# A hybrid two-layer encoder on one core: planner priorities, the place of a neighbourhood unit, key lows in zero-padded tiles, and like matmuls together

## The chip, the cores and the metric

The kernel runs on one core of one Trainium2 chip. The time is that of one execution on the device, in microseconds (us), and smaller is better. One run of the kernel is profiled: each instruction of each engine with its start and its duration. TensorE is called PE in the profile (its weight loads PEld), VectorE DVE, ScalarE ACT, GpSimd POOL, and SyncE, which only issues DMAs here, SP.

## What is computed

512 tokens of width 1024 go through two layers. In each layer the normed input `h` is multiplied by one wide matrix, and its parts go three ways: neighbourhood attention (16 heads on a grid of 8 x 64 tokens), dilated attention (24 heads in three groups with dilations 1, 4 and 16, mixed by their log-sums) and a bidirectional state-space model (24 heads, chunks of 128 tokens). The three results are projected, gated and merged, and a gated embedding is added. All inputs are float32.

```python
for i in range(DEPTH):
    h = rms_norm(x, norm_w[i])
    (qa, ka, va, ga, qb, kb, vb, gb, xbc, z, dt_raw, ua, ub, uc) = [
        h @ w for w in jnp.split(w_in[i], split_idx, axis=1)]
    ya = neighbourhood_attention(split_heads(qa, NA_HEADS), split_heads(ka, NA_HEADS),
                                 split_heads(va, NA_HEADS), na_rpb[i]).reshape(b, s, NA_WIDTH)
    ya = (ya * jax.nn.silu(ga)) @ w_oa[i]
    ...
    yb = dilated_mixture(qbh, kbh, split_heads(vb, DIL_HEADS)).reshape(b, s, DIL_OUT_WIDTH)
    yb = (yb * jax.nn.silu(gb)) @ w_ob[i]
    yc = mamba2_bidirectional(xbc, z, dt_raw, conv_w[i], conv_b[i], a_log[i], dt_bias[i],
                              d_skip[i], ssm_norm_w[i]) @ w_oc[i]
    merged = jax.nn.sigmoid(ua) * ya + jax.nn.sigmoid(ub) * yb + jax.nn.sigmoid(uc) * yc
    x = x + merged @ w_out[i]
    gate = jax.nn.sigmoid(rms_norm(x, ple_norm_w[i]) @ w_ple_gate[i])
    x = x + (p[i] @ w_ple[i]) * gate
return rms_norm(x, final_norm_w)
```

## The kernel before

**Two steps.** The kernel is first recorded and then ordered. `Emit` calls engine methods in program order; each call becomes a `Node` with a number `i`, its engine, its tiles and its predecessors (`Recorder.add`, L222). `Recorder.schedule` (L267) then plays the program through with a table of costs (`cost`, L151) and gives each engine a fixed order of its own; `emit` writes the instructions in that order. On the chip every engine works through its order strictly from front to back and waits at whatever isn't ready. All instructions are written from one place, so nearly all rows of the profile carry L261, and the names of the tiles tell them apart.

**How the planner chooses** (L309 to L340). Each time an engine is free in its play, it takes from the ready nodes the one with the lowest number, if that lies within 2500 places of the first node not yet placed (`WINDOW`) and if `fits` (L392) finds room in the pools for the tiles that it is the first to use. The pools: up to 55 tiles of 2 KB per partition with the tag `t` (`NT`, L432), three each of `raw`, `whi` and `wlo`, and in PSUM three `pj`, two `sc`, two `tr` and one `av` (L440).

**Matmuls in three terms.** Weights come as float32 blocks of 128 x 1024 on SP's queue (`fetch`, L444). `block` (L450) splits each into a high part `whi` (ACT copies with rounding) and a low part `wlo` (DVE subtracts); activations are split likewise (`hh` and `hl`, `yh` and `yl`). A product is then three matmuls, high by high, low by high and high by low (`mm3`, L460). A projection (`proj`, L469) is a block, 24 matmuls of 512 columns into one `pj` tile, and its reader on ACT or DVE.

**The stages of a layer** stand in `ORDER` (L1248), one word for each: `N0` to `N3` are neighbourhood units of four heads (`na_unit`, L1074), `S0` to `S3` state-space groups (`ssm_group`, L760), `O0` and `O1` the halves of the output product of the state-space path (`out_c`, L848), `G` its gates, `D0` and `D1` halves of the dilated attention (`dil_half`, L887), `A` and `B` the merges, and `L` the stores that were put off (`stores`, L1243). Before them stand the norm and the rows of dt (`dt_rows`, L656), behind them `tail` (L1181).

**Scores.** `stack` (L1109) builds for a pair of heads two query tiles `qs` (64 rows of high part, 64 of low part for each head), two key tiles `ks` (the high part twice), and one tile `kl` that holds the low parts of the keys, head 0 in rows 0 to 63 and head 1 in rows 64 to 127. `scores` (L969) makes for two heads and two blocks one matmul over all 128 rows of `qs` and `ks`, and then one over the 64 rows that a head owns in `kl`. The softmax follows on DVE and ACT, four transposes on PE (`turn`, L983) and the product with the values into `av`, whose matmuls write 64 rows of PSUM for each head.

**A state-space pair** (`ssm_pair`, L776) is long on DVE: four convolution steps `cv`, the products `cx`, `z` and `eb`, the states `ent`, and `y`.

**The end of a dilated half** (L920 to L960): the factors of the mixture are worked out on 4 rows (`M`, `mt`, `dn`), stored to memory (`fd`), fetched again spread over 64 rows each (`f`), and multiplied into `o` on DVE.

Of the kernel before, what the change touches and what calls it, by code (L numbers as in the profile page):

```python
# [11 lines left out]
F32 = mybir.dt.float32  # L12
F32R = mybir.dt.float32r
AF = mybir.ActivationFunctionType
ALU = mybir.AluOpType
# [105 lines left out]
class Node:  # L121
    __slots__ = ("i", "eng", "method", "args", "kw", "tiles", "pred", "succ", "cost", "new", "dma", "table", "fetch", "issue",
                 "npred", "ready", "done", "rank")

# [26 lines left out]
def cost(n, eng):  # L151

    args = list(n.args) + list(n.kw.values())
    lazy = [v for v in args if isinstance(v, Lazy)]
    out = n.kw.get("out", n.kw.get("out_", n.args[0] if n.args else None))
    if not isinstance(out, Lazy):
        out = lazy[0]
    free = 1
    for o, k, s in out.box[1:]:
        free *= k  # L160
    if n.dma:
        return 4.0 * free * out.box[0][1] / 360.0
    if eng == "tensor":
        if n.method == "transpose":
            return 107.0
        if lazy[1].base.dtype == F32R:
            return (0.418 * free + 13.5) * (0.6 if lazy[1].box[0][1] == 64 else 1.0)
        if out.box[0][1] <= 64:
            return 54.0 if out.box[0][0] >= 64 else 1.72 * max(free, 64)
        if lazy[1].box[0][1] == 64:  # L170
            return 240.0
        return 1.75 * max(free, 124)
    psum = any(v.base.pool.space == "PSUM" for v in lazy)
    ptr = sum(1 for v in lazy if v.box[1:] and all(k == 1 for o, k, s in v.box[1:]))
    if eng == "scalar":
        return (51 if psum else 93) + 93 * ptr + free / 1.2
    if eng == "vector":
        if n.method == "reciprocal":
            return 64 + 6.27 * free
        if n.method == "tensor_tensor_reduce":  # L180
            ptr = 0
        half = n.method in ("tensor_copy", "tensor_scalar", "memset") and not psum
        return (64 + 61 * ptr + (free / 2 if half else free)) / 0.96
    if n.method == "memset":
        return 60 + free / 1.2
    if n.method == "tensor_copy":
        return 280 + free / 1.2
    if n.method == "tensor_mul" and any(v.box[-1][1] == 1 for v in lazy):
        return 1000.0
    return 160 + 2.08 * free  # L190


class Recorder:
# [28 lines left out]
    def add(self, eng, method, args, kw):  # L222
        n = Node()
        n.i, n.eng, n.method, n.args, n.kw = len(self.nodes), eng, method, args, kw
        n.dma = method == "dma_start"
        n.fetch = n.dma and isinstance(kw["out"], Lazy) and kw["out"].base.pool.space != "DRAM"
        named = dict(kw)
# [7 lines left out]
        for group, wr in ((rest, False), (outs, True)):  # L235
            for ap in group:
# [9 lines left out]
                if wr and (whole or all(o == 0 and k == sz for (o, k, s), sz in zip(ap.box, t.shape))):  # L246
                    h[:] = [x for x in h if x[0] is n]
                h.append((n, ap.box, wr))
        n.issue = 625.0 if n.dma and any(scattered(v) for v in (kw["out"], kw["in_"])) else 450.0
        n.table = None  # L250
        if method == "activation":
            f = args[2]
            n.table = "sqrt" if f == AF.Sqrt else "exp" if f in (AF.Exp, AF.Tanh) else None
        self.nodes.append(n)

    def emit(self, tc):
        order = self.schedule()
        with tc.manual_schedule():
            for n in order:
                f = lambda v: v.real() if isinstance(v, Lazy) else v  # L260
                getattr(getattr(self.real, n.eng), n.method)(*[f(a) for a in n.args],  # L261
                                                             **{k: f(v) for k, v in n.kw.items()})

    WINDOW = 2500
    AHEAD = 600

    def schedule(self):  # L267
# [15 lines left out]
        assert not over, over  # L283
        seen = set()
        for n in nodes:
            n.new = []
            n.npred = len(n.pred)
            n.ready = 0.0
            for m in n.pred:
                m.succ.append(n)  # L290
            for t, wr in n.tiles.items():
                t.left += 1
                if t not in seen:
                    seen.add(t)
                    if t.tag:
                        n.new.append(t)
        avail = {q: [] for q in self.QUEUE}
        wait = {q: [] for q in self.QUEUE}
        for n in nodes:
            if n.npred == 0:  # L300
                for e in FLEX.get(n.eng, (n.eng,)):
                    heapq.heappush(avail[e], n.i)
        clock = dict.fromkeys(self.QUEUE, 0.0)
        busy = dict.fromkeys(self.QUEUE, 0.0)
        dge = dma = now = 0.0
        table, drain = None, False
        events, order = [], []
        front = 0
        scheduled = [False] * len(nodes)  # L309
        while len(order) < len(nodes):  # L310
# [3 lines left out]
            for q in avail:  # L314
# [3 lines left out]
                while w and w[0][0] <= now:  # L318
                    heapq.heappush(av, heapq.heappop(w)[1])
                skipped, n = [], None  # L320
                while av:
                    i = av[0]
                    if i > front + self.WINDOW:
                        break
# [3 lines left out]
                    if not (nodes[i].dma and i > front + self.AHEAD) and self.fits(nodes[i], free, front):  # L328
                        n = nodes[i]
                        break  # L330
                    skipped.append(i)
                    if len(skipped) > 24:
                        break
                for i in skipped:
                    heapq.heappush(av, i)
                if n is None:
# [5 lines left out]
                n.cost = cost(n, q)  # L342
                for t in n.new:
                    free[t.tag] -= 1
                    self.live[t.tag][front:n.i] += 1
                if n.dma:
# [7 lines left out]
                else:  # L354
# [4 lines left out]
                    if q == "tensor":  # L359
                        half = n.cost in (54.0, 1.72 * 128)  # L360
                        c += 84.0 if drain and not half else 0.0
                        drain = half
                    clock[q] = n.done = now + c
# [28 lines left out]
    def fits(self, n, free, front):  # L392

        if not n.new:
            return True
        need = {}
        for t in n.new:
            need[t.tag] = need.get(t.tag, 0) + 1
        for k, v in need.items():
            if free[k] < v or (front < n.i and self.live[k][front:n.i].max() + v > self.caps[k]):  # L400
                return False
        return True


# [8 lines left out]
class Emit:  # L413
# [17 lines left out]

    NT = 55  # L432

# [16 lines left out]
    def block(self, spec, ncols):  # L450
# [4 lines left out]
        lo = self.wp.tile([128, 1024], F32R, tag="wlo", bufs=3, name=self.name("wlo"))  # L455
        nc.scalar.copy(hi[:, :ncols], raw[:, :ncols])
        nc.vector.tensor_sub(lo[:, :ncols], raw[:, :ncols], hi.bitcast(F32)[:, :ncols])
        return hi, lo
# [118 lines left out]
    def constants(self):  # L577
# [14 lines left out]
        self.rst = c(C_RST, S)  # L592
        self.eps = c(C_EPS, 1)

    def load_constants(self, i):
# [40 lines left out]
    def norm_h(self):  # L636
# [7 lines left out]
        for k in range(8):  # L644
# [3 lines left out]
            nc.vector.tensor_sub(self.hl[k][:, 0:S], h, self.hh[k][:, 0:S].bitcast(F32))  # L648
            nc.scalar.copy(self.hh[k][:, S:576], self.hh[k].bitcast(F32)[:, 0:64])
            nc.scalar.copy(self.hl[k][:, S:576], self.hl[k].bitcast(F32)[:, 0:64])  # L650
            if self.layer:
# [317 lines left out]
    def scores(self, pair, q, k, kl):  # L969


        nc = self.nc
        sc = [self.ps("sc", (128, 2, 256)) for _ in range(2)]
        for h in range(2):
            for ii in range(2):
                nc.tensor.matmul(sc[h][:, ii], q(h, pair, ii), k(h, pair, ii), start=ii == 0, stop=False)
        for ii in range(2):
            for h in range(2):
                own = slice(64 * h, 64 * h + 64)
                nc.tensor.matmul(sc[h][:, ii], q(h, pair, ii)[own], kl(pair, ii, own), start=False, stop=ii == 1)  # L980
        return sc
# [11 lines left out]
    def dil_near(self, q, k, kl, st, hl):  # L993
# [6 lines left out]
        for b in range(2):  # L1000
            sc = self.scores(b, lambda h, b, ii: q[h][:, block(2 * b + ii)], lambda h, b, ii: k[h][:, keys(2 * b + ii)],
                             lambda b, ii, own: kl[own, keys(2 * b + ii)])
            Ps = []
# [105 lines left out]
    def stack(self, qp, kp, scale=1.0, perm=lambda t: t, view=lambda t: t, eng=None):  # L1109
# [6 lines left out]
        ks = [self.t(dtype=F32R, nm="ks") for _ in range(2)]  # L1116
        kl = self.t(dtype=F32R, nm="kl")
        for h in range(2):
# [3 lines left out]
            if scale == 1.0:  # L1122
                nc.scalar.copy(ks[h][a], kp[a])
                eng.tensor_sub(kl[a], kp[a], ks[h].bitcast(F32)[a])
            else:
                nc.scalar.activation(ks[h][a], kp[a], AF.Copy, scale=scale)
                nc.vector.scalar_tensor_tensor(kl[a], kp[a], scale, ks[h].bitcast(F32)[a], ALU.mult, ALU.subtract)
        for h in range(2):
# [9 lines left out]
    def na_pair(self, q, k, kl, P):  # L1138
# [10 lines left out]
        for b in range(2):  # L1149
            sc = self.scores(b, lambda h, b, jj: q[h][:, 256 * b + 128 * jj:256 * b + 128 * jj + 128],  # L1150
                             lambda h, b, jj: win(k[h], 2 * b + jj), lambda b, jj, own: win(kl[own], 2 * b + jj))
            mx = self.small((128, 2, 2), "nmx")
# [89 lines left out]

    def stores(self):  # L1243
        for dst, src in self.late:
            self.nc.gpsimd.dma_start(out=dst, in_=src)
        self.load_constants(2)

    ORDER = ("N0 L S0 N1 S1 N2 S2 O0 S3 O1 G D0 N3 D1 A B",  # L1248
             "N0 L S0 N1 S1 N2 S2 O0 S3 O1 G D0 N3 D1 A B")

# [142 lines left out]
```

## Time and profile before

| | us |
|---|---|
| median of 3 runs | 2452.09 (2450.15 to 2454.11) |
| the profiled execution | 2453.53 |
| its span in the trace | 2451.6 |
| DVE: weight splits `wlo` of 1024 columns, 322 | 392.8 |
| ACT: weight splits `whi` of 1024 columns, 322 | 337.9 |
| PE: matmuls `sc<-kl,qs` of 64 rows, 192 | 42.9 busy |

Busy times are sums of durations. Matmuls overlap each other, so a matmul of 512 columns has a mean duration of 402 ns although the next one starts much sooner; paces are therefore read from the starts of neighbouring rows. A value in square brackets behind a row of the order of time is the idle time of the engine before it and what ended it. A row with xN stands for N instructions in a run. The mean granted clock of PE is 0.982 of full speed. The rows on which the argument rests are quoted in the prediction.

### The profile page before, as it was taken

To read this page: it belongs to the slowest core of one execution; us is meant where nothing else is said; L and a number is where in the kernel's file an instruction comes from. 1 tells how busy PE (TensorE), PEld (TensorE's weight loads), DVE (VectorE), ACT (ScalarE), POOL (GpSimd) and SP (SyncE) were. 2 spreads that over 40 slices of the span, in tenths; PEclk is the share of its full clock that TensorE was granted. 3 is DMA by queue.
4 is the path that set the end of the run, shared out by engine and by line. 5 is a ranking of instruction groups with operands and counts; after the bars stand their busy time and mean duration, and the time that the engine had idled before them with its cause. 6 is when DMAs were issued, how large, how long until landed. Compare 5 with 4: busy or idle time off the path is not lost. (4 is left out here: it accounts for less than half of the span.)

```text
span 2451.6 us, 33345 instructions
## 1 busy us (share of the span) xinstructions
PE 2350.0 (96%) x12480; PEld 1928.1 (79%) x12480; DVE 1642.3 (67%) x3227; ACT 1122.5 (46%) x2148; POOL 215.0 (9%) x380
## 2 busy tenths in 40 slices
PE   7999899989998999999999998999899989999998
PEld 6677788878877877788877777788788778777888
DVE  6797978784465556535687878797735663665357
ACT  5636354433355445324465453644234554562245
POOL 1202020000001000200021110210000020002000
PEclk9999999999999999999999999999999999999999
DMA  6625252423214221533355442523322242116333
GB/s 229 162 88 164 86 149 76 136 80 103 86 61 104 89 78 61 172 116 105 109 170 145 117 142 90 148 88 113 101 93 71 73 124 76 66 61 170 107 110 129
DMA packets 111377, 272.74 MB, mean 111 GB/s; under 512 B 39360, under 2 KB 45984, under 8 KB 111216
## 3 DMA queue, kind: packets, MB, share of 16 engines
q1 hardware_dynamic: 56464, 189.73, 23.4%
q0 software_dynamic: 50400, 76.69, 11.8%
q10 hardware_dynamic: 4352, 4.20, 0.5%
q8 instruction: 98, 1.61, 0.3%
q14 instruction: 63, 0.52, 0.1%
HBM read 257.08 MB, written 13.21 MB: 110 GB/s over the span
## 5 line engine op out<-in xcount | busy, mean ns | idle before, releaser
L261 PE MATMUL pj<-hh,whi 128*128 128x512 f32 x1744 | 700.4, 402 | 3.8 <-ACT hh L261 3.8
L261 PE MATMUL pj<-hl,whi 128*128 128x512 f32 x1744 | 700.7, 402 | 1.4 <-DVE hl L261 1.4
L261 PE MATMUL pj<-hh,wlo 128*128 128x512 f32 x1728 | 693.1, 401 | 8.6 <-DVE wlo L261 8.6
L261 ACT CAST whi<-raw 128x1024 fp32r<-128x1024 f32 (+2 forms) x360 | 368.1, 1024 | 702.2 <-PE pj L261 545.2
L261 DVE TENSOR_TENSOR wlo<-raw,whi 128x1024 fp32r<-128x1024 f32 (+2 forms) x358 | 425.7, 1191 | 377.5 <-ACT whi L261 372.5
L261 PEld LDWEIGHTS pj<-hl,whi 128*128 128x128 f32 x1744 | 330.6, 190 | 79.9 <-issue 8.8
L261 PEld LDWEIGHTS pj<-hh,whi 128*128 128x128 f32 x1744 | 331.0, 190 | 78.4 <-issue 7.0
L261 PEld LDWEIGHTS pj<-hh,wlo 128*128 128x128 f32 x1728 | 326.9, 189 | 83.5 <-DVE wlo L261 10.2
L261 PE MATMUL pj<-yh,wlo 128*128 128x512 f32 (+1 forms) x576 | 213.3, 372 | 0.6 <-DVE wlo L261 0.6
L261 PE MATMUL pj<-yl,whi 128*128 128x512 f32 (+1 forms) x576 | 212.7, 370 | 0.0
L261 PE MATMUL pj<-yh,whi 128*128 128x512 f32 (+1 forms) x576 | 211.9, 369 | 0.6 <-ACT th L261 0.6
L261 PE MATMUL pj<-whi,hh 128*128 128x256 f32 (+1 forms) x448 | 139.4, 314 | 11.0 <-ACT th L261 7.1
L261 PE MATMUL pj<-wlo,hh 128*128 128x256 f32 (+1 forms) x448 | 139.7, 313 | 6.6 <-DVE wlo L261 6.6
L261 PE MATMUL pj<-whi,hl 128*128 128x256 f32 (+1 forms) x448 | 138.2, 311 | 0.0
L261 PEld LDWEIGHTS pj<-yh,wlo 128*128 128x128 f32 x576 | 109.9, 191 | 19.8 <-DVE wlo L261 1.4
L261 PEld LDWEIGHTS pj<-yh,whi 128*128 128x128 f32 x576 | 109.6, 190 | 18.6 <-ACT th L261 1.5
L261 PEld LDWEIGHTS pj<-yl,whi 128*128 128x128 f32 x576 | 109.5, 190 | 17.9 <-issue 0.3
L261 DVE SCALAR_TENSOR_TENSOR cv<-cx,cwh,cv 128x510 f32<-128x510 f32 (+1 forms) x160 | 119.3, 746 | 5.5 <-ACT cv L261 4.2
L261 PEld LDWEIGHTS pj<-whi,hh 128*128 128x128 f32 x448 | 96.0, 215 | 15.9 <-ACT th L261 8.4
L261 PEld LDWEIGHTS pj<-wlo,hh 128*128 128x128 f32 x448 | 97.5, 218 | 9.3 <-DVE wlo L261 8.3
L261 ACT ACTIVATE p<-p,nm 128x128 f32<-128x128 f32 (+2 forms) x192 | 80.1, 420 | 39.6 <-DVE nm L261 39.6
L261 PEld LDWEIGHTS pj<-whi,hl 128*128 128x128 f32 x448 | 97.4, 218 | 0.5 <-issue 0.3
(214 smaller groups left out, 3476.5 us busy)
## 6 DMA issues: line engine op xcount, KB each, us to landing
raw<-wt SPq DMA_DIRECT2D x322, 512.0 KB, 3.3
nb<-nab POOLq DMA_DIRECT2D x32, 384.0 KB, 4.6
af<-acd POOLq DMA_DIRECT2D x48, 256.0 KB, 6.0
ab<-acd POOLq DMA_DIRECT2D x48, 256.0 KB, 6.2
raw<-wt SPq DMA_DIRECT2D x32, 384.0 KB, 3.0
eb<-ead POOLq DMA_DIRECT2D x48, 192.0 KB, 9.6
vw<-vd POOLq DMA_DIRECT2D x56, 128.0 KB, 5.0
f<-fd POOLq DMA_DIRECT2D x24, 256.0 KB, 12.8
```

Source lines behind the costliest of these rows:

```text
L261: getattr(getattr(self.real, n.eng), n.method)(*[f(a) for a in n.args], **{k: f(v) for k, v in n.kw.items()})
```

## The change

1. The planner sorts ready nodes by a rank instead of their number. The rank of a weight split (`whi`, `wlo`) is its number less 300 (`EARLY`), that of an instruction outside PE that touches PSUM its number less 60 (`DRAIN`), and that of all others the number.
2. Each matmul gets a mode: `half` (64 rows contracted), `pair` (64 rows written), `wide` (float32r) or `full` (float32). PE looks through up to 12 ready nodes of other modes for one of the mode that it is in, and takes that one if its rank lies less than 60 behind the best (`STAY`, `NEAR`). The planner's table counts 45 or 95 ns for a change of mode, and other costs for some matmuls.
3. `kl` leaves the pool `t`: there are two fixed pairs of tiles, used in turn, one tile for each head, with zeros in the 64 rows that the head doesn't own. The second matmul of `scores` runs over all 128 rows, and its loop stands inside the loop over heads.
4. `NT` goes from 55 to 51.
5. The copies of the first 64 columns of `hh` and `hl` behind column 512, which only the near dilated values read, move from `norm_h` to `stores`.
6. In `ORDER`, `N3` moves from between `D0` and `D1` to between `S3` and `O1`.

```diff
+        n.split = False
+        n.drain = eng != "tensor" and any(isinstance(v, Lazy) and v.base.pool.space == "PSUM"
+                                          for v in list(args) + list(kw.values()))
...
+        n.mode = None
+        if eng == "tensor":
+            w = args[1]
+            n.mode = ("half" if w.box[0][1] == 64 else "pair" if args[0].box[0][1] == 64 else
+                      "wide" if w.base.dtype == F32R else "full")
...
+    EARLY = 300
+    DRAIN = 60
+    STAY, NEAR = 12, 60
     WINDOW = 2500
...
+            n.rank = n.i - (self.EARLY if n.split else self.DRAIN if n.drain else 0)
...
-                    i = av[0]
-                    if i > front + self.WINDOW:
+                    r, i = av[0]
+                    if r > front + self.WINDOW:
                         break
                     heapq.heappop(av)
                     if scheduled[i]:
                         continue
                     if not (nodes[i].dma and i > front + self.AHEAD) and self.fits(nodes[i], free, front):
-                        n = nodes[i]
+                        if q == "tensor" and nodes[i].mode != mode and tries < self.STAY:
+                            if n is None or nodes[i].rank < n.rank:
+                                n = nodes[i]
+                            tries += 1
+                            held.append(i)
+                            continue
+                        if n is None or nodes[i].mode == mode and r < n.rank + self.NEAR:
+                            n = nodes[i]
+                        else:
+                            held.append(i)
                         break
...
                     if q == "tensor":
-                        half = n.cost in (54.0, 1.72 * 128)
-                        c += 84.0 if drain and not half else 0.0
-                        drain = half
+                        c += 0.0 if n.mode == mode else 45.0 if {n.mode, mode} == {"wide", "full"} else 95.0
+                        mode = n.mode
...
-    NT = 55
+    NT = 51
...
-        nc.scalar.copy(hi[:, :ncols], raw[:, :ncols])
-        nc.vector.tensor_sub(lo[:, :ncols], raw[:, :ncols], hi.bitcast(F32)[:, :ncols])
+        for n in (nc.scalar.copy(hi[:, :ncols], raw[:, :ncols]),
+                  nc.vector.tensor_sub(lo[:, :ncols], raw[:, :ncols], hi.bitcast(F32)[:, :ncols])):
+            n.split = True
...
+        self.nkey = 0
+        self.keylow = [[self.cp.tile([128, S], F32R, name=f"kl{i}_{h}") for h in range(2)] for i in range(2)]
+        for pair in self.keylow:
+            for h in range(2):
+                self.nc.gpsimd.memset(pair[h].bitcast(F32)[64 - 64 * h:128 - 64 * h], 0.0)
...
-            nc.scalar.copy(self.hh[k][:, S:576], self.hh[k].bitcast(F32)[:, 0:64])
-            nc.scalar.copy(self.hl[k][:, S:576], self.hl[k].bitcast(F32)[:, 0:64])
...
-        for ii in range(2):
-            for h in range(2):
-                own = slice(64 * h, 64 * h + 64)
-                nc.tensor.matmul(sc[h][:, ii], q(h, pair, ii)[own], kl(pair, ii, own), start=False, stop=ii == 1)
+            for ii in range(2):
+                nc.tensor.matmul(sc[h][:, ii], q(h, pair, ii), kl(h, pair, ii), start=False, stop=ii == 1)
...
-        kl = self.t(dtype=F32R, nm="kl")
+        kl = self.keylow[self.nkey % 2]
+        self.nkey += 1
...
-                eng.tensor_sub(kl[a], kp[a], ks[h].bitcast(F32)[a])
+                eng.tensor_sub(kl[h][a], kp[a], ks[h].bitcast(F32)[a])
...
     def stores(self):
+        nc = self.nc
+        for h in self.hh + self.hl:
+            nc.scalar.copy(h[:, S:576], h.bitcast(F32)[:, 0:64])
...
-    ORDER = ("N0 L S0 N1 S1 N2 S2 O0 S3 O1 G D0 N3 D1 A B",
-             "N0 L S0 N1 S1 N2 S2 O0 S3 O1 G D0 N3 D1 A B")
+    ORDER = ("N0 L S0 N1 S1 N2 S2 O0 S3 N3 O1 G D0 D1 A B",
+             "N0 L S0 N1 S1 N2 S2 O0 S3 N3 O1 G D0 D1 A B")
```

More of the change, by code (lines that the diff above doesn't have):

```diff
@@ L121 @@
 class Node:
-    __slots__ = ("i", "eng", "method", "args", "kw", "tiles", "pred", "succ", "cost", "new", "dma", "table", "fetch", "issue",
-                 "npred", "ready", "done", "rank")
+    __slots__ = ("i", "eng", "method", "args", "kw", "tiles", "pred", "succ", "cost", "dma", "table", "fetch", "issue",
+                 "npred", "ready", "done", "rank", "split", "drain", "mode")
 LATENCY = {"PE": {"PE": 0.0, "*": 197.0}, "ACT": {"ACT": 63.0, "PE": 271.0, "POOL": 159.0, "*": 142.0},
@@ L166, in cost @@
         if lazy[1].base.dtype == F32R:
-            return (0.418 * free + 13.5) * (0.6 if lazy[1].box[0][1] == 64 else 1.0)
+            return 111.0 if lazy[1].box[0][1] == 64 else 0.418 * free + 13.5
         if out.box[0][1] <= 64:
@@ L170, in cost @@
         if lazy[1].box[0][1] == 64:
-            return 240.0
+            return 136.0
         return 1.75 * max(free, 124)
@@ L254, in add @@
         self.nodes.append(n)
+        return n
     def emit(self, tc):
@@ L283, in schedule @@
         assert not over, over
-        seen = set()
+        self.first, self.placed = first, set()
         for n in nodes:
-            n.new = []
             n.npred = len(n.pred)
+            n.rank = n.i - (self.EARLY if n.split else self.DRAIN if n.drain else 0)
             n.ready = 0.0
@@ L292, in schedule @@
                 t.left += 1
[L293 to L296, printed above, removed]
         avail = {q: [] for q in self.QUEUE}
@@ L301, in schedule @@
                 for e in FLEX.get(n.eng, (n.eng,)):
-                    heapq.heappush(avail[e], n.i)
+                    heapq.heappush(avail[e], (n.rank, n.i))
         clock = dict.fromkeys(self.QUEUE, 0.0)
@@ L305, in schedule @@
         dge = dma = now = 0.0
-        table, drain = None, False
+        table, mode = None, None
         events, order = [], []
@@ L318, in schedule @@
                 while w and w[0][0] <= now:
-                    heapq.heappush(av, heapq.heappop(w)[1])
-                skipped, n = [], None
+                    i = heapq.heappop(w)[1]
+                    heapq.heappush(av, (nodes[i].rank, i))
+                skipped, n, held, tries = [], None, [], 0
                 while av:
-                    i = av[0]
-                    if i > front + self.WINDOW:
+                    r, i = av[0]
+                    if r > front + self.WINDOW:
                         break
@@ L333, in schedule @@
                         break
-                for i in skipped:
-                    heapq.heappush(av, i)
+                for i in skipped + [i for i in held if n is None or i != n.i]:
+                    heapq.heappush(av, (nodes[i].rank, i))
                 if n is None:
@@ L342, in schedule @@
                 n.cost = cost(n, q)
-                for t in n.new:
+                for t in self.new(n):
+                    self.placed.add(t)
                     free[t.tag] -= 1
-                    self.live[t.tag][front:n.i] += 1
+                    self.live[t.tag][front:first[t]] += 1
                 if n.dma:
@@ L392, in fits, with new @@
     def fits(self, n, free, front):
[L394 to L397, printed above, removed]
+        need, until = {}, {}
+        for t in self.new(n):
             need[t.tag] = need.get(t.tag, 0) + 1
+            until[t.tag] = max(until.get(t.tag, 0), self.first[t])
         for k, v in need.items():
-            if free[k] < v or (front < n.i and self.live[k][front:n.i].max() + v > self.caps[k]):
+            if free[k] < v or (front < until[k] and self.live[k][front:until[k]].max() + v > self.caps[k]):
                 return False
         return True
+    def new(self, n):
+        return [t for t in n.tiles if t.tag and t not in self.placed]
 class RecEngine:
@@ L1001, in dil_near @@
             sc = self.scores(b, lambda h, b, ii: q[h][:, block(2 * b + ii)], lambda h, b, ii: k[h][:, keys(2 * b + ii)],
-                             lambda b, ii, own: kl[own, keys(2 * b + ii)])
+                             lambda h, b, ii: kl[h][:, keys(2 * b + ii)])
             Ps = []
@@ L1123, in stack @@
                 nc.scalar.copy(ks[h][a], kp[a])
-                eng.tensor_sub(kl[a], kp[a], ks[h].bitcast(F32)[a])
+                eng.tensor_sub(kl[h][a], kp[a], ks[h].bitcast(F32)[a])
             else:
                 nc.scalar.activation(ks[h][a], kp[a], AF.Copy, scale=scale)
-                nc.vector.scalar_tensor_tensor(kl[a], kp[a], scale, ks[h].bitcast(F32)[a], ALU.mult, ALU.subtract)
+                nc.vector.scalar_tensor_tensor(kl[h][a], kp[a], scale, ks[h].bitcast(F32)[a], ALU.mult, ALU.subtract)
         for h in range(2):
@@ L1150, in na_pair @@
             sc = self.scores(b, lambda h, b, jj: q[h][:, 256 * b + 128 * jj:256 * b + 128 * jj + 128],
-                             lambda h, b, jj: win(k[h], 2 * b + jj), lambda b, jj, own: win(kl[own], 2 * b + jj))
+                             lambda h, b, jj: win(k[h], 2 * b + jj), lambda h, b, jj: win(kl[h], 2 * b + jj))
             mx = self.small((128, 2, 2), "nmx")
```

## The prediction

> **What bounds the kernel now.** The head of the page first: the span, and each engine's busy time and share of it.
>
> ```profile
> span 2451.6 us, 33345 instructions
> PE 2350.0 (96%) x12480; PEld 1928.1 (79%) x12480; DVE 1642.3 (67%) x3227; ACT 1122.5 (46%) x2148; POOL 215.0 (9%) x380
> ```
>
> PE is the bound: nothing else is near it. But busy PE time isn't work at full pace, so I looked for time that PE loses in two places: where it stands idle, and where it changes from one shape of matmul to another. The view of stretches gives the first. Its columns are the stretch, its length, busy time of PE, PEld, DVE, ACT and POOL (instructions), granted PE clock, DMA share, GB/s.
>
> ```profile
> 146.00:172.00 26.00, 21.20 (x113) 17.11 (x112) 26.00 (x47) 10.79 (x18) 3.78 (x6) 0.96 0.40 112
> 274.00:306.00 32.00, 25.30 (x138) 20.65 (x137) 30.59 (x53) 11.37 (x19) 3.76 (x6) 0.90 0.37 114
> 516.00:538.00 22.00, 15.39 (x76) 11.76 (x72) 21.07 (x45) 5.26 (x11) 3.09 (x11) 0.78 0.20 64
> 766.00:806.00 40.00, 33.06 (x150) 27.63 (x149) 26.27 (x38) 16.06 (x25) 10.52 (x16) 0.87 0.57 130
> 1012.00:1024.00 12.00, 8.59 (x26) 6.54 (x25) 8.71 (x14) 1.56 (x2) 4.81 (x9) 0.72 0.95 276
> ...
> 1356.00:1382.00 26.00, 21.20 (x121) 17.11 (x120) 26.00 (x46) 10.80 (x18) 3.77 (x6) 1.00 0.40 111
> 1483.00:1515.00 32.00, 25.32 (x140) 20.54 (x138) 30.13 (x52) 11.38 (x19) 3.76 (x6) 0.89 0.39 120
> 1724.00:1746.00 22.00, 15.26 (x83) 11.73 (x79) 21.12 (x44) 5.71 (x11) 2.96 (x12) 0.78 0.22 65
> 1974.00:2014.00 40.00, 33.55 (x153) 28.10 (x153) 26.74 (x39) 16.39 (x26) 10.52 (x17) 0.87 0.58 130
> 2220.00:2234.00 14.00, 10.59 (x39) 7.98 (x38) 11.12 (x17) 2.39 (x4) 5.35 (x10) 0.88 0.92 268
> ```
>
> The loss sits at the same five boundaries in each layer: S0 to N1, S1 to N2, S3 to O1, D0 to N3 and D1 to A. PE is idle for 4.8+6.7+6.6+6.9+3.4 = 28.4 us in layer 0 and 4.8+6.7+6.7+6.5+3.4 = 28.1 in layer 1, **56.5 us** in all. The clock falls with the idling: 0.04x26 + 0.10x32 + 0.22x22 + 0.13x40 + 0.28x12 = 17.6 us of clock are missing in layer 0, 15.3 in layer 1; PE is busy for 79% of these stretches, so about **26 us** more are lost there to slow matmuls.
>
> In the first three stretches DVE is full (26.00 of 26, 30.59 of 32, 21.07 of 22 us). In the other two it isn't. The view of waits and DVE's order of time say why.
>
> ```profile
> DVE o L261 <- DMA f<-fd: 40.7, 5, 11.3
> PE pj L261 <- DVE wlo L261: 15.8, 13, 3.4
> PE sc L261 <- DVE kl L261: 12.6, 4, 5.1
> ```
>
> ```profile
> 1015.25 0.69 DVE L261 TENSOR_TENSOR o<-o,f 128x512 f32<-128x512 f32 x1 [11.34 <-DMA f<-fd]
> 1015.86 1.22 DVE L261 TENSOR_TENSOR wlo<-raw,whi 128x1024 fp32r<-128x1024 f32 x1
> ```
>
> At the end of a D half DVE stands at `o`, here for 11.3 us, waiting for the factors' DMA, and the `wlo` that PE needs (in N3 the `kl`, which PE waits 5.1 us for) is queued behind it.
>
> **Key lows.** The order of PE around scores, first a run of four `kl` matmuls, then a run of two (the last row is the last such run).
>
> ```profile
> 70.15 0.64 PE L261 MATMUL sc<-ks,qs 128*128 128x256 f32 x4
> 70.72 0.51 PE L261 MATMUL sc<-kl,qs 64*128 64x256 f32 x4
> 71.16 0.50 PE L261 MATMUL pj<-hh,whi 128*128 128x512 f32 x1
> 71.50 0.39 PE L261 MATMUL pj<-hl,whi 128*128 128x512 f32 x1
> 71.73 0.39 PE L261 MATMUL pj<-hh,wlo 128*128 128x512 f32 x1
> ...
> 72.42 0.40 PE L261 MATMUL sc<-ks,qs 128*128 128x256 f32 x2
> 72.75 0.50 PE L261 MATMUL sc<-kl,qs 64*128 64x256 f32 x2
> 73.19 0.50 PE L261 MATMUL pj<-hh,wlo 128*128 128x512 f32 x1
> ...
> 2153.80 0.50 PE L261 MATMUL sc<-kl,qs 64*128 64x256 f32 x2
> ```
>
> Paces are starts subtracted from starts: a 512-wide full-row matmul takes 0.23 us (71.50 to 71.73). Four `ks` take 0.57, two take 0.33; so two more cost 0.24, 0.12 each, and 0.09 is left over for going over to 64 rows. Then the `kl` run takes 0.44, **whether it holds four or two**, and the first projection matmul after it 0.34, 0.11 too long. A run costs 0.09+0.44+0.11 = 0.64. As 128-row matmuls, four cost 0.48 and two 0.24: a run of four saves 0.16, a run of two 0.40. There are 68 runs of two; 48 calls of `scores` (32 neighbourhood, 16 near dilated) with 4 matmuls each make 192, so the other 56 are 14 runs of four. Saved: 68x0.40 + 14x0.16 = **29 us**, on the bounding engine, with nothing to hide it either way; bounds 8 us (48x0.16, had all been fours) and 29.
>
> The Trainium skill, "TensorEngine Tiling (Array Packing)", Theoretical Speedup, speaks against this edit: a contraction of 64 rows can run two to the array, up to twice as fast, and padding gives that up. The rows bear out half of it: four `kl` take 0.44 us, 0.11 each, no less than a full-row matmul's 0.12.
>
> The lows' tiles are now two fixed pairs in place of one of the pool's, so DVE's `kl` of a pair waits until the scores of the pair before last are over; `wlo` and `z` stand behind it on DVE, and PE behind those. Those scores are a whole pair older, so I take 0; bound 12.6 us, all the waiting for `kl` now. Four fills of zeros at the start lie on POOL (9% busy): 0, at most 4x0.68.
>
> **Like matmuls together.** PE's order around the value products, with the first and last run of two.
>
> ```profile
> 80.16 0.43 PE L261 MATMUL av<-pt,vw 128*64 128x128 f32 x2
> ...
> 83.49 0.40 PE L261 MATMUL pj<-hh,wlo 128*128 128x512 f32 x1
> 83.82 0.43 PE L261 MATMUL av<-pt,vw 128*64 128x128 f32 x2
> 84.18 0.49 PE L261 MATMUL pj<-hh,whi 128*128 128x512 f32 x1
> 84.61 1.09 PE L261 MATMUL av<-pt,vw 128*64 128x128 f32 x14
> 85.62 0.50 PE L261 MATMUL pj<-hl,whi 128*128 128x512 f32 x1
> ...
> 2189.80 0.43 PE L261 MATMUL av<-pt,v 128*64 128x128 f32 x2
> ```
>
> Sixteen are cut into two and fourteen by one projection matmul. Fourteen take 1.01, 0.072 each; the two take 0.36 instead of 0.144, and the matmul between takes 0.43 instead of 0.23: 0.42 us for each cut. There are 89 runs of two; after 41 of them the next `av` comes within five projection matmuls, after most of the others far later. The new rule stays in a mode while a matmul of it is ready within 60 places, which should close the short cuts; where the second half's `pt` isn't ready it can't. I take 45 cuts, **19 us**, between 0 and 37. It holds full-row f32 matmuls back too; that price is the third rival's.
>
> **Splits and drains early, N3 moved.** No instruction comes or goes. Splits go 300 places forward in ACT's and DVE's choice, PSUM readers 60. Where DVE is full, `wlo` now goes ahead of `z`, `cv` and `cx`; PE gets its block, and those chains are late next, each with its PE hop (transposes, states). N3 takes with it two stores on ACT's queue, on POOL's seven `vw` loads and four `nab` loads, and on SP eight weight blocks, past O1's eight, G's eight and D0's. POOL's queue then meets them after S3's `af`, `ab` and `eb` loads and before D0's `fd`. S3 is followed by independent projections, and O1 finds `yc` old; D0 is followed by D1's value projections, which need only splits while DVE stands at `o`. Of 56.5 us idle I take **half, 28**, and of 26 us of slow clock half, **13**: the DVE work of the full stretches remains, and so does the DMA that holds DVE. Bounds: 0 and 82.
>
> The copies of 64 columns go from the norm to after N0: ACT is 46% busy, PE is the cover, I take 0. In both layers there are 32; uncovered, by the 128x128 `p` row below, 32x0.39 = 12.6 us. The pool goes from 55 to 51 tiles: 0 here, the third rival otherwise. The planner's new costs are no instructions.
>
> **The sum.** 2451.6-29-19-28-13 = 2362.6 us of span. The profiled execution took 2453.53, 1.9 more than its span, and lies 1.4 above the median 2452.09; so 2362.6+1.9-1.4 = **2363 us**.
>
> **Rivals.**
> (1) The waits only change place: DVE is full at three boundaries whatever its order, and a plan that fills one hole opens another. Then only the shapes pay: 2452-48 = 2404 (2390 to 2420). For it: 26.00 of 26; against it: PE needs only the split, 1.2 us of DVE for 24 matmuls.
> (2) Padding loses: two 64-row matmuls run side by side as one. By the 0.12 of a full-row matmul, four `kl` would be 0.24, padded 0.48: 48x0.24 = 11.5 us lost instead of 29 gained, 2404. The rule is the one named above; the 0.44 speaks against it.
> (3) Slower: fewer tiles and held-back matmuls starve D. Counted through the code, a D1 half holds up to 45 tiles at once in program order, so 10 are spare for running ahead now and 6 after; and a full-row f32 transpose can be held for 60 places. A dilated unit's softmax is
>
> ```profile
> L261 DVE CUSTOM_DVE_ANT_0 p<-sc,consts 128x128 f32<-128x128 f32 x128 | 29.5, 287 | 27.9 <-PE sc L261 27.9
> L261 ACT ACTIVATE p<-p,nm 128x128 f32<-128x128 f32 x128 | 49.9, 393 | 23.1 <-DVE nm L261 23.1
> ```
>
> 4x0.29 + 4x0.39 = 2.7 us, with both heads about 5 us that PE waits when nothing else is ready. There are 24 units; with the waits as now it decides from 48/5 = 10 units on; at 16 the time is 2452-48+80 = 2484.
> (4) No change: the planner doesn't group and new waits eat the lows: 2452.
> (5) All the boundaries close, and most cuts: 2452-29-30-55-20 = 2318 to 2345.
>
> **Chances.** Forecast (2345 to 2390) 0.45; (1) 0.25; (2) 0.03; (3) 0.10; (4) 0.05; (5) 0.12. A measurement of this kernel can tell about 0.2%, 5 us, from no change. Faster is 0.45+0.25+0.03+0.12 = 0.85, same 0.05, slower 0.10. The range leaves out (3), (4) and the lowest third of (5): 2325 to 2430.
>
> **What would show it.** Lows: no 64x256 `kl` rows, 192 matmuls of 128x256 at 0.12, no 0.44 run. Grouping: few runs of two among `av`, runs of 16 or more. Order: the stretches around S0-N1 and S1-N2 with PE nearly full and the clock at 1.00, and the wait of PE for `wlo` well under 15.8 us; no hole after S3. Wrong would be: new waits of PE for `cv`, `cx`, `z` or `pt` of the old size (rival 1), or holes in D with PE waiting for `p` (rival 3).

## The result, and the profile after

| | before | after |
|---|---|---|
| median, us | 2453.1 (4 runs, 2450.15 to 2454.81) | 2354.06 (4 runs, 2352.89 to 2360.02) |
| ratio | 1 | 0.9602 (0.9583 to 0.9622) |
| span of the profiled execution, us | 2451.6 | 2351.1 |
| PE idle (span less busy), us | 101.6 | 65.0 |
| mean granted clock of PE | 0.982 | 0.991 |

The changed kernel is 4.0% faster, 99 us by the medians; the forecast of 2363 us was 9 us too high. Nearly all rows carry L270 now, where they carried L261 before (L272 in e1 and L276 in e8 are the same line). The head of its page:

```profile
span 2351.1 us, 33495 instructions
PE 2286.1 (97%) x12480; PEld 1900.3 (81%) x12480; DVE 1646.9 (70%) x3227; ACT 1117.0 (48%) x2148; POOL 218.8 (9%) x384
```

Each engine issues as many compute instructions as before (POOL 4 more, the zero fills). PE is busy for 63.9 us less (2350.0 to 2286.1) and idle for 36.6 us less. The first is matmuls that take less time: fewer changes of shape (e1 puts 33.9 us on the key lows alone), and a clock that stays up, 0.991 on average for 0.982. The second is holes. The view of stretches of the changed kernel, in layer 0 (same columns as in the prediction), at S0 to N1, S1 to N2, S3 to N3, D0 to D1 and D1 to A:

```profile
140.00:172.00 32.00, 32.00 (x211) 27.76 (x212) 31.95 (x67) 12.95 (x25) 1.08 (x2) 1.00 0.24 83
262.00:306.00 44.00, 44.00 (x300) 38.51 (x299) 42.74 (x85) 15.37 (x29) 0.41 (x1) 1.00 0.25 85
490.00:540.00 50.00, 49.26 (x305) 42.52 (x304) 42.85 (x97) 22.93 (x43) 7.59 (x13) 1.00 0.40 122
780.00:850.00 70.00, 65.89 (x356) 59.01 (x354) 48.20 (x94) 33.56 (x63) 7.21 (x10) 1.00 0.32 99
930.00:945.00 15.00, 13.81 (x75) 10.00 (x74) 10.09 (x29) 13.74 (x31) 0.00 (x0) 1.00 0.15 49
```

Read the first row against 146 to 172 of before. DVE is as full as it was (31.95 of 32 us), but PE is full too: 32.00 of 32, where it had been busy for 21.20 of 26. The DVE work did not shrink; what PE needs of it now comes first. Idle time at the five boundaries of layer 0 falls from 28.4 to 0+0+0.7+4.1+1.2 = 6.0 us, and the clock is 1.00 in all of them. In layer 1 it falls from 28.1 to 5.8 us. That is 44.7 us less at the boundaries and 36.6 us less in the whole span, so elsewhere PE waits 8.1 us more than before. The view of waits of the changed kernel:

```profile
DVE o L270 <- DMA f<-fd: 43.9, 6, 11.5
...
PE sc L270 <- ACT ks L270: 8.5, 3, 4.9
PE tr L270 <- DVE np L270: 7.5, 4, 3.3
PE sc L270 <- DVE nmx L270: 6.1, 5, 4.6
```

PE's wait for `wlo`, 15.8 us before, is gone from the list. DVE still stands as long for the factors' DMA (43.9 us, 40.7 before), but hardly anything that PE needs stands behind it. Of the 65.0 us that are left, 15.2 lie in the first 40 us and 6.8 behind the last matmul. The three PE rows above are the longest of the other waits. They lie mostly at the beginning of N0 and N1 (the longest at 98.7 and 209.4 us, and at 1260.2 in layer 1), for `ks`, `nmx` and `np`, the keys and the softmax there.

### The profile page after: what moved, and what is told of

Same layout as the page of the kernel before. It is cut to its first block, busy times and chain, and to the rows that moved or that the text cites. A ratio compares the mean times of both kernels' runs of the same rounds, so it can differ in the third digit from the quotient of the medians.

```text
span 2351.1 us, 33495 instructions
## 1 busy us (share of the span) xinstructions
PE 2286.1 (97%) x12480; PEld 1900.3 (81%) x12480; DVE 1646.9 (70%) x3227; ACT 1117.0 (48%) x2148; POOL 218.8 (9%) x384
## 3 DMA queue, kind: packets, MB, share of 16 engines
q0 software_dynamic: 50400, 76.69, 11.8%
## 5 line engine op out<-in xcount | busy, mean ns | idle before, releaser
L270 ACT CAST whi<-raw 128x1024 fp32r<-128x1024 f32 (+2 forms) x360 | 368.4, 1023 | 699.8 <-PE pj L270 550.3
L270 PE MATMUL pj<-hl,whi 128*128 128x512 f32 x1744 | 693.2, 397 | 2.9 <-DVE hl L270 2.9
L270 PE MATMUL pj<-hh,whi 128*128 128x512 f32 x1744 | 691.7, 397 | 1.5 <-ACT hh L270 1.5
L270 PE MATMUL pj<-hh,wlo 128*128 128x512 f32 x1728 | 687.4, 398 | 0.1
L270 DVE TENSOR_TENSOR wlo<-raw,whi 128x1024 fp32r<-128x1024 f32 (+2 forms) x358 | 426.3, 1191 | 338.4 <-ACT whi L270 334.5
L270 PEld LDWEIGHTS pj<-hl,whi 128*128 128x128 f32 x1744 | 330.4, 189 | 70.8 <-issue 4.8
L270 PEld LDWEIGHTS pj<-hh,whi 128*128 128x128 f32 x1744 | 330.6, 190 | 66.1 <-issue 2.2
L270 PEld LDWEIGHTS pj<-hh,wlo 128*128 128x128 f32 x1728 | 326.7, 189 | 69.7 <-issue 7.4
L270 PE MATMUL pj<-yh,whi 128*128 128x512 f32 (+1 forms) x576 | 212.5, 369 | 0.0
L270 PE MATMUL pj<-yh,wlo 128*128 128x512 f32 (+1 forms) x576 | 211.2, 367 | 0.0
L270 PE MATMUL pj<-yl,whi 128*128 128x512 f32 (+1 forms) x576 | 210.9, 366 | 0.0
L270 PE MATMUL pj<-whi,hh 128*128 128x256 f32 (+1 forms) x448 | 136.0, 305 | 2.0 <-ACT v L270 2.0
L270 PE MATMUL pj<-whi,hl 128*128 128x256 f32 (+1 forms) x448 | 135.0, 303 | 1.2 <-DVE hl L270 1.2
L270 PE MATMUL pj<-wlo,hh 128*128 128x256 f32 (+1 forms) x448 | 135.9, 304 | 0.0
L270 PEld LDWEIGHTS pj<-yh,wlo 128*128 128x128 f32 x576 | 108.6, 189 | 18.1 <-issue 0.7
L270 PEld LDWEIGHTS pj<-yh,whi 128*128 128x128 f32 x576 | 108.6, 189 | 17.8 <-issue 1.0
L270 PEld LDWEIGHTS pj<-yl,whi 128*128 128x128 f32 x576 | 108.8, 189 | 16.8
L270 DVE SCALAR_TENSOR_TENSOR cv<-cx,cwh,cv 128x510 f32<-128x510 f32 (+1 forms) x160 | 119.5, 747 | 2.4 <-ACT cv L270 0.3
L270 PEld LDWEIGHTS pj<-whi,hh 128*128 128x128 f32 x448 | 93.5, 209 | 3.8 <-ACT v L270 2.4
L270 ACT ACTIVATE p<-p,nm 128x128 f32<-128x128 f32 (+2 forms) x192 | 80.2, 420 | 34.2 <-DVE nm L270 34.2
L270 PEld LDWEIGHTS pj<-whi,hl 128*128 128x128 f32 x448 | 93.3, 209 | 2.6 <-DVE hl L270 1.4
L270 PEld LDWEIGHTS pj<-wlo,hh 128*128 128x128 f32 x448 | 93.9, 210 | 1.8 <-issue 1.2
```

## The experiments

All stand against the kernel before, measured on the same chip; as the medians of that kernel were 2453 to 2458 us on the chips used, I compare ratios. 0.001 is 2.5 us; the changed kernel is 0.9602.

| run | ratio, 95% interval | against the changed kernel, us |
|---|---|---|
| e1 key lows over 64 rows | 0.9684 (0.9665 to 0.9703) | +20 |
| e2 splits without lead | 0.9911 (0.9893 to 0.9929) | +76 |
| e3 no grouping by mode | 0.9627 (0.9605 to 0.9650) | +6, unclear |
| e4 N3 at its old place | 0.9855 (0.9828 to 0.9882) | +62 |
| e5 both of e2 and e4 | 1.0065 (1.0050 to 1.0080) | +114 |
| e6 before, with key lows and 51 tiles | 1.0062 (1.0045 to 1.0078) | |
| e7 drains without lead | 0.9667 (0.9653 to 0.9682) | +16 |
| e8 value products held | 0.9522 (0.9504 to 0.9540) | -20 |
| e9 before, with 51 tiles | 1.0164 (1.0146 to 1.0181) | |
| e10 47 tiles | 0.9650 (0.9634 to 0.9665) | +12 |
| e11 splits' lead and N3 alone | 0.9786 (0.9763 to 0.9808) | +45 |

**e1: key lows over 64 rows, nothing else moved.** The planner sees the changed kernel; only at the writing of the instructions the operands are cut.

```diff
+                args = [n.args[0]] + [a[n.rows] for a in n.args[1:]] if n.rows else n.args
...
-                nc.tensor.matmul(sc[h][:, ii], q(h, pair, ii), kl(h, pair, ii), start=False, stop=ii == 1)
+                n = nc.tensor.matmul(sc[h][:, ii], q(h, pair, ii), kl(h, pair, ii), start=False, stop=ii == 1)
+                n.rows = slice(64 * h, 64 * h + 64)
```

> The order of every engine as in the changed kernel; only the key-low matmuls contract the 64 rows that their head owns instead of 128. Theory (shapes cost PE directly): 96 runs of two such matmuls, each with 0.09 us to get into the mode, 0.44 for the run and 0.11 to get out, in place of 0.24: 96 x 0.40 = 38 us more, 2392 us. Rival (two 64-row matmuls run side by side, so the padding is a loss): 2343 to 2354 us. Rival (PE has slack there): under 2365 us.

Measured: 0.9684, 20 us more than the changed kernel (24 by the spans). First the changed kernel's order of PE, then that of e1, at the same scores:

```profile
222.92 0.39 PE L270 MATMUL pj<-hh,wlo 128*128 128x512 f32 x1
223.15 0.40 PE L270 MATMUL sc<-ks,qs 128*128 128x256 f32 x2
223.38 0.41 PE L270 MATMUL sc<-kl,qs 128*128 128x256 f32 x2
223.63 0.40 PE L270 MATMUL sc<-ks,qs 128*128 128x256 f32 x2
223.87 0.41 PE L270 MATMUL sc<-kl,qs 128*128 128x256 f32 x2
```

```profile
221.65 0.40 PE L272 MATMUL sc<-ks,qs 128*128 128x256 f32 x2
221.98 0.51 PE L272 MATMUL sc<-kl,qs 64*128 64x256 f32 x2
222.41 0.51 PE L272 MATMUL sc<-ks,qs 128*128 128x256 f32 x2
222.85 0.50 PE L272 MATMUL sc<-kl,qs 64*128 64x256 f32 x2
223.28 0.50 PE L272 MATMUL pj<-hh,whi 128*128 128x512 f32 x1
223.62 0.39 PE L272 MATMUL pj<-hl,whi 128*128 128x512 f32 x1
```

Over 128 rows two low matmuls take 0.25 us (223.38 to 223.63); over 64 rows 0.43 (221.98 to 222.41), with 0.09 ahead of them and 0.11 behind. The cost of one run is as I had it, 0.38 for 0.40. Yet 96 of them make 20 to 24 us and not 38. The page says where the rest is:

```profile
span 2375.3 us, 33491 instructions
PE 2320.0 (98%) x12480; PEld 1913.6 (81%) x12480; DVE 1649.4 (69%) x3227; ACT 1118.4 (47%) x2148; POOL 218.7 (9%) x384
```

PE is busy for 2320.0-2286.1 = 33.9 us more but idle for 55.3 instead of 65.0. Read the other way, of the time that the better shape frees, 9.7 us turn into waits for DVE and ACT. Of the rivals, padding as a loss falls; slack is true in part.

**e2: the splits without their lead** (`EARLY = 0`).

> Weight splits keep their own place in the planner's choice (EARLY 0 instead of 300); all else as in the changed kernel. Theory (DVE-full boundaries, splits first): the holes after S0 and S1 come back, 11.5 us per layer with some 4 us of slow clock, and one after S3: 25 to 45 us more, 2380 to 2400 us, with PE waiting for wlo again. Rival (the move of N3 and the drains closed the holes): under 2362 us.

Measured: 0.9911, 76 us more, well beyond what either theory said. The stretches at S0 to N1, S1 to N2 and S3 to N3, and PE's longest wait:

```profile
144.00:172.00 28.00, 21.60 (x118) 17.31 (x117) 28.00 (x49) 11.46 (x19) 3.77 (x6) 0.94 0.36 112
272.00:300.00 28.00, 21.56 (x115) 17.38 (x114) 27.69 (x49) 10.21 (x18) 3.77 (x6) 0.91 0.36 111
508.00:530.00 22.00, 13.39 (x62) 11.89 (x61) 19.56 (x40) 6.06 (x11) 0.00 (x0) 0.70 0.21 66
```

```profile
PE pj L270 <- DVE wlo L270: 16.9, 12, 4.0
```

The first two holes of before are back (6.4 us each; 4.8 and 6.7 before), and S3 to N3 is a hole as well, 8.6 us at a clock of 0.70. So with N3 moved but without the lead these three stay open. In all, PE is idle for 2431.4-2313.1 = 118.3 us, 53.3 more than in the changed kernel, and its mean clock is 0.980.

**e3: no grouping by mode** (`STAY, NEAR = 0, 60`).

> PE takes the lowest rank whatever its mode (STAY 0 instead of 12). Theory: the runs of value products go from 142 back to about 190, 49 x 0.3 us = 15 us more, 2369 us. Rival (grouping pays nothing, or holding matmuls back costs as much as it gives): 2349 to 2359 us.

Measured: 0.9627, 6 us more, with an interval that overlaps the changed kernel's. The runs of value products on PE, counted along the order of time, are 149 here, 142 in the changed kernel and 191 before: grouping is good for 7 of the 49 that went. A miss of mine.

**e4: N3 back between D0 and D1.**

```diff
-    ORDER = ("N0 L S0 N1 S1 N2 S2 O0 S3 N3 O1 G D0 D1 A B",
...
+    ORDER = ("N0 L S0 N1 S1 N2 S2 O0 S3 O1 G D0 N3 D1 A B",
...
```

> N3 goes back between D0 and D1; all else as in the changed kernel. Theory: the holes at S3 to O1 and D0 to N3 (6.6 + 6.9 us per layer and slow clock) come back in part, since splits now go first: 15 to 40 us more, 2369 to 2394 us. Rival (splits first closes these holes by itself): 2349 to 2360 us.

Measured: 0.9855, 62 us more, beyond the range again. The stretch at S3 to O1, first in e4, then in e5 (the same kernel without the lead) and in e9 (the kernel before with 51 tiles), and PE's longest wait in e4:

```profile
495.00:537.00 42.00, 23.75 (x123) 18.31 (x122) 27.66 (x55) 9.10 (x15) 6.36 (x17) 0.78 0.22 62
```

```profile
515.00:557.00 42.00, 31.98 (x171) 24.90 (x170) 34.97 (x73) 13.28 (x23) 6.26 (x17) 0.92 0.29 85
```

```profile
520.00:560.00 40.00, 25.16 (x127) 19.25 (x128) 29.95 (x67) 9.13 (x17) 5.33 (x12) 0.84 0.22 71
```

```profile
PE av L270 <- DVE z L270: 29.5, 8, 9.5
```

PE is idle in this hole for 18.3 us. Before, it was 6.6, but with 55 tiles; with 51 tiles the kernel before has 14.8 here (e9), so tiles alone can make this hole long. The fair neighbour is e5, which differs by the lead alone: 10.0 us. So the lead adds 8.3 us here. My reading is that splits first let PE run through S3's projections and leave the state-space chain behind, and that `O1` needs the end of that chain (its last `yc`). The work left is a chain and not a full engine: DVE is busy for 27.66 of the 42 us, and 8.8 us of its idle time end with the DMAs of `eb` and `ab`. Whether the planner could have placed other work there isn't shown. With N3 behind S3 PE is busy for 49.26 of 50 us there, as the changed kernel's third row shows.

**e5: both undone.**

> Both undone at once: splits without their lead (EARLY 0) and N3 back between D0 and D1. Alone, the one cost 76 us and the other 62 against the changed kernel's 2354. Theory (the two need each other: splits first let PE run past the DVE work of S3, and only N3 behind S3 gives it something to run to): without both the holes of before stand, 6.6 us at S3, no more, and the time is that of before less the key lows and the rest of the shapes, 2415 to 2440 us, no slower than with one undone. Rival (two separate gains that add up): 2354 + 76 + 62 = 2492 us.

Measured: 1.0065, slower than the kernel before, which neither theory had. Still the four corners, with all the rest of the change in place, answer the question: neither 1.0065, lead alone (e4) 0.9855, N3 alone (e2) 0.9911, both 0.9602. One by one they give 0.0210 and 0.0154, together 0.0463: **0.010, 24 us, are there only when both are** (with the four intervals taken together, some 14 to 34 us). N3 alone does pay, then: e5 has a hole of 8.0 us between 795 and 825 us, at D0 to N3, 7.9 of it one wait for `kl`, and e2 has no such wait. And the rest of the change, alone, costs 0.65%. Why, the next runs ask.

**e6: the kernel before, with the key lows and their 51 tiles. e9: the kernel before with 51 tiles (`NT = 51`) and nothing else. e10: the changed kernel with 47 tiles (`NT = 47`).**

> The kernel before with the zero-padded key lows and 51 tiles alone. Theory: the 82 runs of 64-row matmuls go, 68 x 0.40 + 14 x 0.16 = 29 us at most; at the changed kernel a third of such time was taken up by waits that shrank, so 18 to 29 us less than before, ratio 0.988 to 0.993. Rival (4 tiles fewer, or a new order, eat it): ratio 0.997 or more.

> The kernel before with 51 tiles instead of 55, nothing else; it answers what made the key lows alone slower (ratio 1.0062 where 0.99 was expected). Theory (fewer tiles keep the planner from running ahead; the lows' own gain of some 20 to 29 us was more than eaten): 35 to 45 us slower than before, ratio 1.014 to 1.018. Rival (a faster PE only meets the same DVE-full stretches sooner, and tiles are beside the point): ratio 0.998 to 1.003.

> The changed kernel with 47 tiles instead of 51. Theory (splits first, with N3 behind S3, give PE work without running far ahead, so the tiles no longer bind): within 6 us of the changed kernel, 2348 to 2360 us. Rival (a tile is worth as much here as in the kernel before): 2385 us or more.

Measured: e6 1.0062, a miss; e9 1.0164, as the theory said. Four tiles cost the kernel before **40 us**. Between e9 and e6 lies the edit to the lows, with 51 tiles in the pool in both: 1.0164-1.0062 = 0.0102, **25 us** gained. (In e6 `kl` no longer takes a tile of the pool, so e6 has a little more room. It doesn't show in the waits: by the pages PE is busy for 26.2 us less than in e9, and idle for 136.9 us instead of 133.9.) PE's longest waits in e9, then in e6:

```profile
PE pj L261 <- DVE wlo L261: 31.8, 16, 7.0
PE av L261 <- DVE z L261: 17.4, 8, 3.4
```

```profile
PE pj L261 <- DVE wlo L261: 29.1, 10, 7.1
PE av L261 <- DVE z L261: 18.3, 8, 3.4
```

Before, these were 15.8 and 3.8 us. That fits a planner that can lay less work ahead of the stretches where DVE is full; e9 changes nothing but the tiles. e5 and e6 come out the same on the same chip, 1.0065 and 1.0062, though e5 has the drains, the grouping and the planner's new costs besides: without the lead and N3 these bring nothing that can be told. In the changed kernel four tiles more taken away cost 12 us (e10, 0.9650), between the two expectations: fewer than the 40 of before, but not nothing.

**e7: drains without lead** (`DRAIN = 0`).

> Instructions that read PSUM keep their own place (DRAIN 0 instead of 60). Theory: PE waits a little more for PSUM tiles that ACT or DVE has still to read: 3 to 15 us more, 2357 to 2369 us. Rival (splits first is all that counts): 2349 to 2357 us.

Measured: 0.9667, 16 us more, a bit over the range. PE's longest waits:

```profile
PE pj L270 <- DVE wlo L270: 11.0, 2, 7.4
PE sc L270 <- DVE kl L270: 9.2, 2, 5.4
```

Mostly not waits for PSUM, as I had thought: `wlo` and `kl` are late twice each, once in each layer. PE's wait for ACT's `v`, which reads a `pj` tile of PSUM, rises too, but only from 2.0 to 7.1 us.

**e8: the first value product held back.** In the planner alone, the first matmul of an `av` tile also depends on the second head's operands.

```diff
+    def hold(self, n, tiles):
+        for t in tiles:
+            for m, box, wr in self.hist[t.base]:
+                if wr and m is not n:
+                    n.pred[m] = True
...
-                nc.tensor.matmul(yd[64 * h:64 * h + 64, c], xt[:, c, 64 * h:64 * h + 64], zs[h][:, c],
-                                 start=True, stop=True)
+                n = nc.tensor.matmul(yd[64 * h:64 * h + 64, c], xt[:, c, 64 * h:64 * h + 64], zs[h][:, c],
+                                     start=True, stop=True)
+                if c == h == 0:
+                    nc.hold(n, zs)
```

(and likewise after the first `av` matmul in `dil_half` and `na_unit`)

> The changed kernel; the planner takes the first value product of a tile only when the operands of both heads are there. In the changed kernel 56 of 61 runs of two are such first products, which wait for the second head's transposes or z, cut off by projections; by the plan the runs of value products go from 142 to 64. Theory (a run costs PE 0.3 to 0.42 us to go in and out): 78 x 0.3 = 23 us less, half of it to 23 net of waits, 2331 to 2343 us. Rival (first products early let the rest follow sooner, and holding them delays y and what hangs on it): 2349 us or more.

Measured: 0.9522, 20 us less than the changed kernel and within the theory's range, **2338 us: the fastest version here**. (A float32 matmul shows as two instructions, so a run of two is one product.) First the changed kernel, where the first product is alone and the other seven follow 3.8 us later; then e8, and the head of its page:

```profile
260.95 0.43 PE L270 MATMUL av<-z,tT 128*64 128x128 f32 x2
261.32 0.50 PE L270 MATMUL pj<-hh,whi 128*128 128x512 f32 x1
261.65 0.40 PE L270 MATMUL pj<-hl,whi 128*128 128x512 f32 x1
...
264.70 1.09 PE L270 MATMUL av<-z,tT 128*64 128x128 f32 x14
```

```profile
140.27 1.09 PE L276 MATMUL av<-z,tT 128*64 128x128 f32 x16
141.29 0.50 PE L276 MATMUL pj<-hl,whi 128*128 128x512 f32 x1
```

```profile
span 2331.4 us, 33486 instructions
PE 2255.7 (97%) x12480; PEld 1888.5 (81%) x12480; DVE 1642.2 (70%) x3227; ACT 1113.4 (48%) x2148; POOL 218.0 (9%) x384
```

One product alone takes 0.37 us, the other seven 1.02, and all eight together 1.02 as well. The runs of value products fall from 142 to 64. PE's busy time falls by 30.4 us, 0.39 for each run that goes, and its idle time rises from 65.0 to 75.7: as in e1, about a third of what the shape gives is taken back by waits.

**e11: the lead of the splits and N3, with the old key lows, 55 tiles, no lead for drains and no grouping** (the edits of e3 and e7, and the code of before in `scores` and `stack`).

> Of the change only the lead of the splits, the place of N3, the later column copies and the planner's costs; key lows over 64 rows in a pool of 55 tiles, no drains first, no grouping. Theory (these two carry most of it, the rest adds 24 for the lows, 20 for the drains, 6 for grouping, at most): 2375 to 2405 us. Rival (nothing works without the rest): 2440 us or more.

Measured: 0.9786, which is 53 us of the 98 that the whole change gives. These two, with the column copies and the planner's new costs, carry half of it; the rest of the change, which alone makes the kernel slower (e5), adds 45 us on top of them.

## Why the prediction was right or wrong

The forecast was 2363 us and the measurement 2354.06. The direction and the main mechanism held (splits first, with N3 behind S3, keep PE fed); of the other steps, grouping had the wrong cause, and the tiles were wrong. That the total came within 9 us is in part luck, since errors went both ways. By the steps:

- **Splits early and N3 moved, 41 us (28 idle, 13 clock): right in kind, too small.** This is the mis-sized term. I took half of the holes; at the five boundaries of both layers 56.5 us of idling became 11.8, and the clock there is 1.00 throughout. In time the two are worth 53 us with the lows, drains and grouping left out and 55 tiles (e11), and 114 with the rest in place (e5 against the changed kernel). e2 and e4 show why half was wrong: the two parts aren't two chances at the same holes. The lead closes the holes after S0 and S1 and makes the one after S3 longer (18.3 us for 10.0 in e5), and N3 fills that.
- **Drains** I had put into the same term without a price of their own. They are worth 16 us in the changed kernel (e7).
- **Key lows, 29 us: the run's cost was right, the term a little large.** 20 us in the changed kernel (e1), 25 in the kernel before with 51 tiles (e6 against e9). What I had left out is that PE waits more when it gets faster: 9.7 us in e1, 3.0 in e6.
- **Like matmuls together, 19 us: the price of a cut was about right (0.42 us; 0.39 by e8), the cause wrong.** Runs of value products did fall, from 191 to 142, but grouping by mode accounts for 7 of these and for some 6 us that can't be told from nothing (e3). What made the others fall stays open: there are 148 runs in e5 and 162 in e11, and both have the planner's new costs, which weren't tried alone. I had read short cuts as the planner's preference for lower numbers. Most of those left are dependences: the first head's product is ready, the second's isn't. e8 closes them, and it takes a held matmul to do so.
- **51 tiles, nothing: wrong as a step.** Four tiles cost 40 us in the kernel before (e9), and four more cost 12 in the changed one (e10). In the change itself `kl` leaves the pool with them, so its share may be smaller. What 55 tiles would give in the changed kernel isn't tried. The loss lies in the sum against the underrated first term and the drains, and that is the luck in the total.
- **The third rival** had the right mechanism, tiles that limit how far the planner runs ahead, and the wrong place: not D but the ends of the S stages, with PE waiting for `wlo` and `z`. With neither the lead nor N3's move the kernel would indeed have come out slower (e5). The first rival (waits only change place) is what e4 shows, where the lead works without N3 behind S3; in the changed kernel it holds for N0 and N1 alone. The second (padding loses) falls to e1.
- The moved column copies and the planner's new costs weren't tried alone. Nor was one more part of the change, which the list above the prediction leaves out: `fits` now counts a pool tile at the first instruction that is placed on it, where it had counted it at the lowest-numbered one that uses it. That POOL's queue would cope with N3's loads at the new place is borne out only by the lack of a hole there.

## What to carry to other kernels

When a fixed order starves the bounding engine, look at what the full engine does first, and then at what is left for the bounding one to do when the debt comes due: a priority and a place for independent work can be worth more together than the sum of both, and one of them alone can make a hole longer. Price buffers by an experiment that takes a few away and does nothing else; a good edit that costs four tiles was a loss here until the order needed them less. When a comparison changes two things, look for the run that changes one: the hole after S3 grew from 6.6 to 18.3 us, but only 8.3 of that was the lead. A short run of an odd matmul shape can cost as much as a longer one (0.44 us for two or four `kl`, 1.02 for seven or eight value products), so let the first wait for the rest. Expect some of the gain to come back as waits: about a third in e1 and e8, a tenth in e6.

## What the runs showed of the hardware

**Matmuls over 64 rows.** Two low matmuls over 64 rows of one head take 0.43 us (e1, 221.98 to 222.41), and four of two heads took 0.44 in the kernel before. Row by row in the trace of the kernel before, the second matmul of such a run starts 0.22 us after the first (72.755 and 72.979), where full-row ones of the same 256 columns start 0.12 apart. The weight loads (PEld) show the difference. Between full-row matmuls the next load starts 3 ns after the matmul ahead of it and lies beside it (223.146 and 223.149 in the changed kernel). The load of the second 64-row matmul starts only 0.107 us after the first (72.862), and its matmul another 0.117 later. It looks as if in this run the load and the matmul took turns. Two heads' matmuls, on different halves of the rows, do run side by side: in a run of four they start 3 ns apart (70.718 and 70.721). A pair then takes 0.22 us, against 0.24 for two full-row matmuls, and the changes of shape around the run decide for padding.

The Trainium skill, "TensorE: Matmul & The Clock Gate", Why this matters for your kernels, has a single matmul over 32 rows take the same time as one over 128, and puts the gain in matmuls that run at once. No run here has 32 rows of float32r; with 64 rows a single one takes 0.22 us from start to start against 0.12, with the load that isn't hidden, and matmuls of two heads do run at once, started 3 ns apart.

**Value products, which write 64 rows each.** Eight took as long as seven, 1.02 us (e8 and the changed kernel). The trace shows why: instructions of the two heads start in pairs, 7 ns apart (264.864 and 264.871), and from pair to pair it is 0.109 us. When the first product has gone ahead alone, the last of the seven has no partner, and its two instructions take two places of their own (265.410 and 265.519).
